# Gate products of two attentions on another engine, and a third buffer for the input tiles of a LayerNorm

## The chip, the cores and the metric

One core of a Trainium2 chip runs the whole layer. Five engines work beside each other, each with its own queue of instructions that it takes strictly in order: PE multiplies matrices (PEld loads its weights), DVE (VectorE) and ACT (ScalarE) do elementwise work, POOL (GpSimd) does slower elementwise work, and SP issues the transfers (DMA). An instruction that waits on a semaphore holds everything behind it in its queue. The metric is the device time of one execution in microseconds (us), the median of repeated runs.

## The reference

One layer of a streaming encoder, in float32: 1024 frames of width 1024, eight heads of width 64 in each of two attentions. Cut to what matters here:

```python
h = layer_norm(x, ln_in_g, ln_in_b)
proj = h @ w_in[0] + b_in[0]
a_q, a_k, a_v, a_z, b_cq, b_ckv, b_kr, b_z, g_a, g_b = split(proj)
ya = chunked_relpos_attention(a_q, a_k, a_v, rel_bias)   # 64-frame chunks, 8 chunks to the left
ya = (ya * silu(a_z)) @ w_proj_a
cq, ckv = rms_norm(b_cq), rms_norm(b_ckv)                # low-rank queries, keys and values
yb = chunk_causal_attention(q_full(cq), k_full(ckv, b_kr), v(ckv))
yb = (yb * silu(b_z)) @ w_proj_b
out = (sigmoid(g_a) * ya + sigmoid(g_b) * yb) @ w_out
h = layer_norm(2 ** 0.25 * h + out, ln_post_g, ln_post_b)
```

The gate products of the title are `ya * silu(a_z)` and `yb * silu(b_z)`.

## The kernel before

Every float32 matrix product is made of three passes over a high and a low part of each operand (`three`, L173 to L175); a helper `split` makes the parts (L131 on ACT for the high one, L132 on DVE or POOL for the low one).

**Opening.** x comes in eight tiles of 128 frames. For each, `ln_tile` takes statistics on DVE (L342, L344), the reciprocal root on POOL (L128, tile `rs`), centres and scales on DVE (L347, L350, in place in `xt`), stores the tile to `h_d` (L351), and turns it with PE transposes (L357, tile `hps`) into `hT`, high part by ACT (L358) and low part by DVE (L359). PE meanwhile multiplies the tiles that are ready into values (`v_tile`, tile `vps`). The x tiles live in a ring `x4` of four buffers, two of which hold the LayerNorm's rows `lng` and `lnb`; so two x tiles are in flight, and the load of tile 2 waits until tile 0 is stored. The same ring later holds the tiles `ct` of the low-rank projections, the tables `csT` and the tiles `qrt` of the rotated queries; a ring `str` of two half-size buffers holds `krh`, `krl`, `qrh` and `qrl`.

**Low-rank projections.** `c_tile` multiplies into `cps` (two PSUM buffers), DVE adds a bias (L407), ACT squares into the same PSUM tile (L410, L411), and only then may PE reuse it. DVE also computes the sine tables there (L466 to L494).

**Attention.** 64 steps for each of the two attentions (8 heads by 8 blocks of 128 queries). A step: PE scores (L712, L713, or L809 to L811), DVE evicts them with the row minimum (L717 or L816), ACT exponentiates (L828), DVE takes a reciprocal (L830, L831), ACT and DVE make the high and low half of the probabilities (L835, L836), SP issues a transposing transfer `pT<-p` (L838), and three (first attention) or two steps later PE multiplies `pT` with the values (L850, tile `y`). After every fourth step `finish_y` joins two halves of `y` into `yt` (L741 on ACT, L742 on DVE), and `finish_z` multiplies it by its gate `sz` (L748) and stores it to `y_d` (L750), 28 of 32 times; the last four are split on chip. Between the steps PE works through the dense projections (tile `dn`, weights `wr_c`, `wh_c`, `wl_c`), so that the latency of a step has dense work to hide behind.

**What sets the order.** Nobody writes the queues out: the kernel is traced under a scheduler that simulates a timeline and gives each engine its instructions in the order in which they become ready there. `tc.issue_after(i)` keeps the work inside it behind instruction i. A changed duration or buffer in one place therefore reorders the queues in many.

Of the kernel before, what the change touches and what calls it, by code (L numbers as in the profile page):

```python
# [11 lines left out]
F32R = mybir.dt.float32r  # L12
I32 = mybir.dt.int32
AF = mybir.ActivationFunctionType
ALU = mybir.AluOpType
# [3 lines left out]
P = 128  # L19
# [36 lines left out]
def tile_hybrid_layer(  # L56
# [25 lines left out]
    V, A, G, SY = nc.vector, nc.scalar, nc.gpsimd, nc.sync  # L82
# [220 lines left out]
    p0 = ctx.enter_context(ExitStack())  # L303
    p0w = ctx.enter_context(ExitStack())
    pw = p0.enter_context(tc.tile_pool(name="pw", bufs=1, side="right"))
    px = p0.enter_context(tc.tile_pool(name="px", bufs=4, side="right"))
    ln_p[0] = p0.enter_context(tc.tile_pool(name="ln_p", bufs=6, side="right"))
    pr = p0w.enter_context(tc.tile_pool(name="pr", bufs=8, side="right"))
    if True:
# [13 lines left out]
        lnb = px.tile([P, D], F32, tag="x4", name="lnb")  # L323
# [14 lines left out]
        def ln_tile(j):  # L338
            xt = xts.pop(j)
            st6 = ln_p[0].tile([P, 2, 6], F32, tag="st6", name=f"st6_{j}")  # L340
            for i in range(2):
                V.bn_stats(st6[:, i, :], xt[:, i * 512 : i * 512 + 512])  # L342
            mv = ln_p[0].tile([P, 2], F32, tag="mv", name=f"mv_{j}")
            V.bn_aggr(mv, st6)  # L344
            rs = ln_p[0].tile([P, 1], F32, tag="rs", name=f"rs_{j}")
            i_pool = rsqrt(rs, mv[:, 1:2], 1.0, 1e-5, 1, f"ln{j}")
            V.scalar_tensor_tensor(xt, xt, mv[:, 0:1], lng, op0=ALU.subtract, op1=ALU.mult)  # L347
            for b in range(2) if j == 0 else [slice(0, D)]:
                cs = slice(b * 512, b * 512 + 512) if j == 0 else b
                V.scalar_tensor_tensor(xt[:, cs], xt[:, cs], rs, lnb[:, cs], op0=ALU.mult, op1=ALU.add)  # L350
            SY.dma_start(h_d[j * P : (j + 1) * P, :], xt)  # L351
            sl = slice(j * P, (j + 1) * P)
            pool, tag = ((ps_sc, "sc"), (ps_y, "y"))[j % 2]
            for b in range(2):
                ps = pool.tile([P, 4, P], F32, tag=tag, name=f"hps{j}_{b}")
                for k in range(4):
                    i_pe = T.transpose(ps[:, k, :], xt[:, (4 * b + k) * P : (4 * b + k + 1) * P], ident).ins  # L357
                i_act = A.activation(hT[0][b][:, :, sl], ps, AF.Copy).ins  # L358
                i_dve = V.tensor_tensor(hT[1][b][:, :, sl], ps, f(hT[0][b][:, :, sl]), op=ALU.subtract).ins  # L359
            return i_pool, i_act, i_dve, i_pe  # L360

        dma_last = [None]

# [64 lines left out]
        def c_transpose(q):  # L428
            sl = slice(q * 512, q * 512 + 512)
            for b in range(4):  # L430
# [9 lines left out]
                    A.activation(dh, psf, AF.Copy, scale=g)  # L440
                    V.scalar_tensor_tensor(dl, psf, g, f(dh), op0=ALU.mult, op1=ALU.subtract)
                else:
                    kh = px.tile([32, 512], F32R, tag="str", name=f"krh{q}", bufs=2)
                    kl = px.tile([32, 512], F32R, tag="str", name=f"krl{q}", bufs=2)
                    A.activation(kh, psf[:32, :], AF.Copy)
                    V.tensor_tensor(kl, psf[:32, :], f(kh), op=ALU.subtract)
                    SY.dma_start(kr_d[0][:, sl], f(kh))
# [110 lines left out]
        ln_last = {}  # L558
# [14 lines left out]
        for j in range(2, NT):  # L573
            if j + 1 < NT:
                x_load(j + 1)
            ln_last[j] = ln_tile(j)
            v_tile(0, j - 1, w0)
            v_tile(1, j - 2, w1)
        v_tile(0, 7, w0)
# [42 lines left out]
    def rot_q(csT):  # L622
# [3 lines left out]
        for half in range(2):  # L626
# [7 lines left out]
            for a in range(2):  # L634
# [2 lines left out]
                V.tensor_tensor(t0, pss[a], csT[0][:, sl], op=ALU.mult)  # L637
                V.tensor_tensor(t1, pss[1 - a], csT[1][:, sl], op=ALU.mult)
                V.tensor_tensor(t0, t0, t1, op=ALU.subtract if a == 0 else ALU.add)
                hi = px.tile([P, 512], F32R, tag="str", name=f"qrh{a}{half}", bufs=2)  # L640
                lo = px.tile([P, 512], F32R, tag="str", name=f"qrl{a}{half}", bufs=2)
                split(t0, hi, lo)
                SY.dma_start(qr_d[0][a * P : (a + 1) * P, sl], f(hi))
                SY.dma_start(qr_d[1][a * P : (a + 1) * P, sl], f(lo))
# [2 lines left out]
    with ExitStack() as p1:  # L647
# [97 lines left out]
        def finish_z(pair, mixer, e, half, yt, r):  # L745
            h = 2 * pair.p + e
            sl = slice(half * 512, half * 512 + 512)
            G.tensor_tensor(yt[r, :], yt[r, :], pair.sz[half][r, :], op=ALU.mult)  # L748
            if h < 6 or mixer == 0:
                SY.dma_start(y_d[mixer][h * 64 : h * 64 + 64, sl], yt[r, :])  # L750
            else:
# [426 lines left out]
```

## Time and profile before

| | us |
|---|---|
| median of 3 runs (lowest, highest) | 878.96 (878.48, 880.91) |
| profiled execution, its own time | 874.21 |
| its span, first to last instruction | 872.4 |
| PE busy in the span | 821.9 |
| DVE busy | 592.2 |
| ACT busy | 443.0 |
| POOL busy | 197.6 |

The profiled execution is one run; the 1.8 us between its time and its span lie outside the instructions. PE is the engine to watch: what it waits for is what a change can win. In the rows below, a name in the form `out<-in` gives the tile that is written and those that are read; a bracket `[idle <-releaser]` says how long the engine had stood idle before the instruction and what ended that.

### The profile page before, as it was taken

Reading aid. Unit: us, or ns where it says so; the run is one execution under the profiler, and the core shown is the slowest. Engines: PE = TensorE matmul, PEld = TensorE weight load, DVE = VectorE, ACT = ScalarE, POOL = GpSimd, SP = SyncE. Lnnn points to the kernel's source line nnn. Section 1 sums busy time; section 2 is a strip of 40 time slices with the busy share of each in tenths; the row PEclk is TensorE's granted clock in tenths of the full one; section 3 lists DMA queues with packets and bytes.
Section 4 is the critical chain, followed back from the end, with each engine's and each line's share of the span. In section 5 each row is a group of like instructions: output and inputs, shape, how many; then the busy total and the mean of one; then the engine's idle time right before and its main releaser. Section 6 shows DMA issues by size and latency. Waiting matters only on the chain. (4 is left out here: it accounts for less than half of the span.)

```text
span 872.4 us, 13717 instructions
## 1 busy us (share of the span) xinstructions
PE 821.9 (94%) x4760; PEld 691.5 (79%) x4760; DVE 592.2 (68%) x1351; ACT 443.0 (51%) x857; POOL 197.6 (23%) x205
## 2 busy tenths in 40 slices
PE   5999999998998998999999999999999989999996
PEld 4999898887776876787778778787888778888886
DVE  6899856587686889845565767276637674647755
ACT  4223683476675857755563666366647552322000
POOL 6545630011111113400000521010213131331100
PEclk8999999999999999999999999999999999999999
DMA  6622023476877775674639377746886798541421
GB/s 210 209 106 77 13 62 109 142 149 141 165 138 168 139 178 96 135 202 102 152 96 200 80 166 159 162 102 140 192 199 173 186 217 289 161 151 49 160 94 48
DMA packets 185365, 124.68 MB, mean 143 GB/s; under 512 B 146161, under 2 KB 149745, under 8 KB 185297
## 3 DMA queue, kind: packets, MB, share of 16 engines
q1 hardware_dynamic: 185296, 123.82, 57.0%
q8 instruction: 37, 0.61, 0.3%
q14 instruction: 32, 0.25, 0.1%
HBM read 57.98 MB, written 22.81 MB: 93 GB/s over the span
## 5 line engine op out<-in xcount | busy, mean ns | idle before, releaser
L173 PE MATMUL dn<-hT,wh_c 128*128 128x512 f32 x512 | 204.8, 400 | 2.0 <-ACT g L294 1.3
L175 PE MATMUL dn<-hT,wl_c 128*128 128x512 f32 x512 | 201.5, 394 | 0.0
L174 PE MATMUL dn<-hT,wh_c 128*128 128x512 f32 x512 | 201.4, 393 | 0.0
L748 POOL TENSOR_TENSOR yt<-yt,sz 64x512 f32<-64x512 f32 x32 | 43.6, 1362 | 328.0 <-DVE yt L742 263.8
L173 PEld LDWEIGHTS dn<-hT,wh_c 128*128 128x128 f32 x512 | 97.0, 190 | 20.2 <-ACT g L294 1.8
L175 PEld LDWEIGHTS dn<-hT,wl_c 128*128 128x128 f32 x512 | 96.7, 189 | 20.0
L174 PEld LDWEIGHTS dn<-hT,wh_c 128*128 128x128 f32 x512 | 97.0, 189 | 17.6
L132 DVE TENSOR_TENSOR wl_c<-wr_c,wh_c 128x512 fp32r<-128x512 f32 x64 | 47.8, 746 | 77.4 <-ACT wh_c L131 71.2
L131 ACT ACTIVATE wh_c<-wr_c 128x512 fp32r<-128x512 f32 x64 | 40.2, 629 | 82.4 <-DMA wr_c<-in_wch_dram 63.2
L836 DVE SCALAR_TENSOR_TENSOR p<-sbs,rcs,p 128x128 f16<-128x128 f32 (+3 forms) x64 | 57.1, 901 | 24.2 <-ACT p L835 22.3
L828 ACT ACTIVATE sbs<-sbs,nmb 128x128 f32<-128x128 f32 (+3 forms) x64 | 49.5, 774 | 33.4 <-DVE sbs L816 30.1
L836 DVE SCALAR_TENSOR_TENSOR p<-ss,rcs,p 128x640 f16<-128x640 f32 (+2 forms) x64 | 50.7, 803 | 9.2 <-ACT p L835 8.1
L828 ACT ACTIVATE ss<-ss,nm 128x640 f32<-128x640 f32 (+2 forms) x64 | 44.3, 692 | 23.1 <-DVE nm L717 20.6
L835 ACT ACTIVATE p<-sbs,rcs 128x128 f16<-128x128 f32 (+3 forms) x64 | 48.5, 769 | 12.8 <-ACT sbs L828 6.8
L850 PE MATMUL y<-pT,v16b 128*128 128x128 f16 x576 | 43.7, 222 | 9.8 <-DMA pT<-p 9.8
L175 PE MATMUL ops<-wo,mixT 128*128 128x512 f32 (+1 forms) x144 | 52.9, 367 | 0.0
L850 PEld LDWEIGHTS <-v16b 128*128 128x128 f16 x576 | 33.9, 99 | 23.8 <-issue 22.2
L174 PE MATMUL ops<-wo,mixT 128*128 128x512 f32 (+1 forms) x144 | 52.7, 366 | 0.0
L173 PE MATMUL ops<-wo,mixT 128*128 128x512 f32 (+1 forms) x144 | 51.5, 368 | 0.0
L816 DVE TENSOR_SCALAR_CACHE_REDUCE sbs<-sb 128x128 f32<-128x128 f32 (+3 forms) x64 | 47.9, 754 | 1.3
L717 DVE CUSTOM_DVE_ANT_0 ss<-sa,tb 128x640 f32<-128x640 f32 (+2 forms) x64 | 41.3, 652 | 8.9 <-PE sa L713 5.2
L850 PE MATMUL y<-pT,v16a 128*128 128x128 f16 x480 | 37.4, 220 | 9.6 <-DMA pT<-p 9.6
(248 smaller groups left out, 1847.8 us busy)
## 6 DMA issues: line engine op xcount, KB each, us to landing
wr_c<-in_wch_dram SPq DMA_DIRECT2D x64, 256.0 KB, 3.2
th_d<-g SPq DMA_DIRECT2D x32, 256.0 KB, 2.9
th<-th_d SPq DMA_DIRECT2D x32, 256.0 KB, 3.7
h_d<-xt SPq DMA_DIRECT2D x8, 512.0 KB, 2.6
sX<-sQ SPq DMA_DIRECT2D x16, 256.0 KB, 4.2
sXb<-bQ SPq DMA_DIRECT2D x16, 256.0 KB, 4.3
r<-h_d SPq DMA_DIRECT2D x8, 512.0 KB, 3.6
wor<-in_wo_dram SPq DMA_DIRECT2D x16, 256.0 KB, 3.0
```

The source lines that it names most:

```text
L131: A.activation(hi, raw, AF.Copy)
L132: (eng or V).tensor_tensor(lo, raw, f(hi), op=ALU.subtract)
L173: T.matmul(ps, ah, bh, start=start, stop=False)
L174: T.matmul(ps, ah, bl, start=False, stop=False)
L175: return T.matmul(ps, al, bh, start=False, stop=stop).ins
L717: V.tensor_tensor_reduce(s[:, :n].rearrange("p (b w) -> p b w", b=nb), ps[:, :nb, :w], self.tb[e][:, 640 - n : 640].rearrange("p (b w) -> ...
L748: G.tensor_tensor(yt[r, :], yt[r, :], pair.sz[half][r, :], op=ALU.mult)
L816: V.tensor_scalar(s[:, :n].rearrange("p (b w) -> p b w", b=nb), ps[:, :nb, :w], -B_SCALE, None, op0=ALU.mult, op1=ALU.min, accum_out=nm,)
L828: A.activation(s[:, :n], s[:, :n], AF.Exp, scale=-1.0, bias=nm, accum_out=su)
L835: A.activation(hi, s[:, :n], AF.Copy, scale=rc2)
L836: V.scalar_tensor_tensor(lo, s[:, :n], rc2, hi, op0=ALU.mult, op1=ALU.subtract)
L850: T.matmul(o, v16[:, k0 + k, h % 4, :], pT[:, a * nk + k, :], start=(k == 0 and a == 0), stop=(k == nk - 1 and a == 1))
```

## The change

Three edits. The gate product `yt * sz` moves from POOL to DVE. The ring `x4` gets a fifth buffer, which makes three for x tiles, and the ring `str` goes: `krh`, `krl`, `qrh` and `qrl` take `x4` buffers (the memory is the same). And `ln_tile(j)` for j from 2 on is issued behind the last L350 of tile j-1, so that no statistics of a tile come before the scaling of the one ahead.

```diff
-    px = p0.enter_context(tc.tile_pool(name="px", bufs=4, side="right"))
+    px = p0.enter_context(tc.tile_pool(name="px", bufs=5, side="right"))
@@ ln_tile
-                V.scalar_tensor_tensor(xt[:, cs], xt[:, cs], rs, lnb[:, cs], op0=ALU.mult, op1=ALU.add)
+                i_sc = V.scalar_tensor_tensor(xt[:, cs], xt[:, cs], rs, lnb[:, cs], op0=ALU.mult, op1=ALU.add).ins
-            return i_pool, i_act, i_dve, i_pe
+            return i_pool, i_act, i_dve, i_pe, i_sc
@@ c_transpose
-                    kh = px.tile([32, 512], F32R, tag="str", name=f"krh{q}", bufs=2)
-                    kl = px.tile([32, 512], F32R, tag="str", name=f"krl{q}", bufs=2)
+                    kh = px.tile([32, 512], F32R, tag="x4", name=f"krh{q}")
+                    kl = px.tile([32, 512], F32R, tag="x4", name=f"krl{q}")
@@
         for j in range(2, NT):
             if j + 1 < NT:
                 x_load(j + 1)
-            ln_last[j] = ln_tile(j)
+            with tc.issue_after(ln_last[j - 1][4]):
+                ln_last[j] = ln_tile(j)
@@ rot_q
-                hi = px.tile([P, 512], F32R, tag="str", name=f"qrh{a}{half}", bufs=2)
-                lo = px.tile([P, 512], F32R, tag="str", name=f"qrl{a}{half}", bufs=2)
+                hi = px.tile([P, 512], F32R, tag="x4", name=f"qrh{a}{half}")
+                lo = px.tile([P, 512], F32R, tag="x4", name=f"qrl{a}{half}")
@@ finish_z
-            G.tensor_tensor(yt[r, :], yt[r, :], pair.sz[half][r, :], op=ALU.mult)
+            V.tensor_tensor(yt[r, :], yt[r, :], pair.sz[half][r, :], op=ALU.mult)
```

What moves in the queues, at three places. The first is DVE in the opening (xt_158 is x tile 1, xt_222 tile 2; L342 statistics, L350 scaling):

```order
 L127 TENSOR_SCALAR rst_ln_230<-mv_227 128x1
 L347 SCALAR_TENSOR_TENSOR xt_158<-xt_158,mv_227,lng 128x1024
-L342 BN_STATS st_2_299<-xt_222 128x6
 L350 SCALAR_TENSOR_TENSOR xt_158<-xt_158,rs_229,lnb 128x1024
-L342 BN_STATS st_2_299<-xt_222 128x6
+L342 BN_STATS st_2_299<-xt_222 128x6 x2
 L344 BN_AGGR mv_302<-st_2_299 128x2
```

The first half of tile 2's statistics no longer stands ahead of tile 1's scaling.

The second is SP in the opening (xt_124 is x tile 0, xt_297 tile 3; wv1r are weights of the second value group):

```order
 L121 DMA gkv<-in_kvn_g_dram 128x1
+L316 DMA xt_222<-in_x_dram 128x1024
+L351 DMA h_d<-xt_124 128x1024
 L458 DMA pi_t<-in_pos_dram 128x8
-L351 DMA h_d<-xt_124 128x1024
+L135 DMA wv1r_279<-in_wv_dram 128x512
 L459 DMA fr_t<-in_invf_dram 128x16
-L135 DMA wv1r_279<-in_wv_dram 128x512
 L135 DMA wv1r_283<-in_wv_dram 128x512
-L316 DMA xt_222<-in_x_dram 128x1024
+L316 DMA xt_297<-in_x_dram 128x1024
 L135 DMA wv1r_289<-in_wv_dram 128x512
```

The load of tile 2 now stands ahead of the store of tile 0, and every later x load one place earlier.

The third is DVE in the second attention, around the second product of its first head, before:

```order
L813 MEMSET sb_3_5366 64x64
L816 TENSOR_SCALAR sbs_2_5286,nmb_2_5287<-sb_2_5281 128x384
L742 SCALAR_TENSOR_TENSOR yt_0_1_5276<-y_0_4_5088,us_102,yl_0_1_5275 64x512
L816 TENSOR_SCALAR sbs_3_5371,nmb_3_5372<-sb_3_5366 128x512
L660 TENSOR_TENSOR bK_5173<-bk_1_5189,bK_5173 64x512
L830 TENSOR_SCALAR rcs_1_2_5291<-su_1_2_5289 128x1
```

and after (every line number behind L576 is one higher there):

```order
L743 SCALAR_TENSOR_TENSOR yt_0_1_5276<-y_0_4_5088,us_102,yl_0_1_5275 64x512
L814 MEMSET sb_4_5397 64x64
L831 TENSOR_SCALAR rcs_1_2_5291<-su_1_2_5289 128x1
L817 TENSOR_SCALAR sbs_3_5371,nmb_3_5372<-sb_3_5366 128x512
L749 TENSOR_TENSOR yt_0_1_5276<-yt_0_1_5276,sz_1_5042 64x512
L832 RECIPROCAL rcs_1_2_5291<-rcs_1_2_5291 128x1
L661 TENSOR_TENSOR bQ_5311<-bq_0_5313,bQ_5311 64x512
```

The product (L749) has joined DVE's queue, with an eviction and small work between it and the row that makes `yt`; the reciprocal of the step now stands behind it.

## Rows read from the trace of the kernel before

**Rows 1.** Page, busy us, share of the span and instructions of each engine.
```profile
PE 821.9 (94%) x4760; PEld 691.5 (79%) x4760; DVE 592.2 (68%) x1351; ACT 443.0 (51%) x857; POOL 197.6 (23%) x205
```
**Rows 2.** Stretches: length, busy PE, PEld, DVE, ACT, POOL, clock, DMA share, GB/s.
```profile
0.00:25.00 25.00, 14.49 (x80) 13.50 (x81) 17.17 (x23) 11.68 (x20) 17.34 (x19) 0.86 0.68 220
...
100.00:150.00 50.00, 50.00 (x262) 44.32 (x262) 31.71 (x95) 30.65 (x73) 13.05 (x20) 1.00 0.23 69
...
188.00:400.00 212.00, 198.70 (x1258) 163.64 (x1257) 158.01 (x380) 141.76 (x278) 41.46 (x49) 0.99 0.73 154
400.00:735.00 335.00, 318.92 (x1845) 261.23 (x1845) 206.67 (x512) 189.49 (x346) 55.18 (x47) 0.99 0.68 159
```
**Rows 3.** Timeline of PE: start us, duration us, instruction, [idle before <-releaser].
```profile
20.70 1.97 PE L357 MATMUL hps<-ident,xt 128*128 128x128 f32 x8 [4.53 <-DVE xt L350]
...
89.79 0.45 PE L173 MATMUL cps<-wcch,hT 128*128 128x416 f32 x1 [1.87 <-ACT cps L411]
```
**Rows 4.** Timeline of DVE in the opening.
```profile
15.42 1.28 DVE L347 SCALAR_TENSOR_TENSOR xt<-xt,mv,lng 128x1024 f32<-128x1024 f32 x1
18.09 0.69 DVE L342 BATCH_NORM_STATS2 st<-xt 128x6 f32<-128x512 f32 x1 [1.39 <-DMA xt<-in_x_dram]
18.70 1.95 DVE L350 SCALAR_TENSOR_TENSOR xt<-xt,rs,lnb 128x1024 f32<-128x1024 f32 x1
```
**Rows 5.** Timeline of POOL in the opening.
```profile
15.58 1.53 POOL L128 TENSOR_TENSOR rs<-rst_ln,mhalf 128x1 f32<-128x1 f32 x1 [0.48 <-DVE rst_ln L127]
17.09 2.48 POOL L132 TENSOR_TENSOR wv1l<-wv1r,wv1h 128x512 fp32r<-128x512 f32 x2
```
**Rows 6.** Timeline of PE, three waits in the attentions.
```profile
284.96 0.38 PE L850 MATMUL y<-pT,v16a 128*128 128x128 f16 x4 [2.40 <-DMA pT<-p]
...
337.59 0.42 PE L712 MATMUL sa<-sK,sQ 128*128 128x320 f32 x1 [2.28 <-DVE nm L717]
...
443.16 0.38 PE L809 MATMUL sb<-bK,bQ 128*128 128x320 f32 x1 [1.96 <-DVE sbs L816]
```
**Rows 7.** Busy time by stretch around waits; the granted clock stands third from the end.
```profile
20.00:24.00 4.00, 3.30 (x15) 3.07 (x16) 3.93 (x6) 1.21 (x3) 4.00 (x3) 0.57 0.67 224
282.00:288.00 6.00, 3.60 (x28) 2.93 (x27) 4.53 (x14) 5.07 (x11) 0.00 (x0) 1.00 0.78 119
336.00:340.00 4.00, 2.41 (x8) 2.13 (x9) 3.39 (x10) 2.38 (x5) 0.00 (x0) 0.73 0.42 98
```
**Rows 8.** Timeline of DVE, two later statistics in the opening.
```profile
27.86 1.29 DVE L342 BATCH_NORM_STATS2 st<-xt 128x6 f32<-128x512 f32 x2 [1.33 <-DMA xt<-in_x_dram]
...
39.91 1.29 DVE L342 BATCH_NORM_STATS2 st<-xt 128x6 f32<-128x512 f32 x2 [0.53 <-DMA xt<-in_x_dram]
```
**Rows 9.** Timeline of DVE, first bias of the low-rank projections.
```profile
88.11 0.58 DVE L407 TENSOR_TENSOR ct<-cps,bvc_t 128x416 f32<-128x416 f32 x1
```
**Rows 10.** Groups by line and form: count, busy us and mean ns, idle before.
```profile
L748 POOL TENSOR_TENSOR yt<-yt,sz 64x512 f32<-64x512 f32 x32 | 43.6, 1362 | 328.0 <-DVE yt L742 263.8
...
L132 DVE TENSOR_TENSOR YB<-yt,YB 64x512 fp32r<-64x512 f32 x4 | 2.7, 685 | 1.4 <-ACT YB L131 1.3
```
**Rows 11.** Waits: who waited for what, us in total, times, longest.
```profile
PE y L850 <- DMA pT<-p: 19.4, 23, 2.4
...
SPq L750 <- POOL yt L748: 17.8, 9, 3.7
```
**Rows 12.** Timeline of POOL and of SP around one product.
```profile
227.80 1.29 POOL L748 TENSOR_TENSOR yt<-yt,sz 64x512 f32<-64x512 f32 x1
...
229.12 0.46 SPq L750 DMA_DIRECT2D y_d<-yt  x1
229.68 1.27 SPq L838 DMA_TRANSPOSE pT<-p  x1
```
**Rows 13.** Tile wl_c, durations min/median/max; timeline of DVE beside a product.
```profile
L132 DVE TENSOR_TENSOR wl_c<-wr_c,wh_c x64: 673/692/1679, 80.8 to 647.8; 128x512 fp32r<-128x512 f32 x64
...
214.50 1.58 DVE L132 TENSOR_TENSOR wl_c<-wr_c,wh_c 128x512 fp32r<-128x512 f32 x1
```

## The prediction

> **What bounds the kernel now.** The first view is busy time by engine. PE is busy 821.9 of the 872.4 us of the span, 94% [rows 1]; no other engine comes near it. So the matrix products, which the change leaves alone, are a floor, and the 50 us in which PE stands idle, with the times at which its clock is low, are all that there is to win. The second view, busy time by stretch, says where they are [rows 2]: 10.5 us in the first 25 us, 13.3 us in the first attention (212 less 198.7) and 16.1 us in the second (335 less 318.9), while between 100 and 150 us PE has no gap at all. The third, PE's timeline, says what each gap waits for. In the opening the largest is 4.53 us for the scaling of x tile 1 by DVE, and at 89.79 us there are 1.87 us for ACT, which squares a tile of the low-rank projections [rows 3]. In the attentions most of the gaps end with a transposed tile of probabilities: 23 waits, 19.4 us [rows 11]; others end with an eviction by DVE [rows 6].
>
> The forecast is made as a difference. The profiled execution took 874.21 us, 872.4 of them span, and the median of the three timed runs is 878.96, so this one execution lies 4.75 us below the median; I take the terms from its rows and set the difference against the median.
>
> **The order of statistics, and the third buffer.** In the opening DVE centres tile 1 (start 15.42, 1.28 us, to 16.70), then stands 1.39 us for the arrival of tile 2, takes half of tile 2's statistics (18.09, 0.69 us), and only then scales tile 1, from 18.70 [rows 4]. The scaling needs the root from POOL, which was there at 15.58 + 1.53 = 17.11 [rows 5]. With the statistics behind it, it starts at 17.11: 18.70 - 17.11 = 1.6 us earlier. Its own 1.95 us against the 1.28 us of the centring, an instruction of the same form, could shrink too, since a POOL instruction on two SBUF tiles starts at 17.09 beside it [rows 4, 5]; as that is still there, I keep 1.95 us and hold 0.67 us as a bound. PE has waited for nothing else there, so its first gap falls from 4.53 to 2.9 us. Term: -1.6, between -1.6 and -2.3.
>
> The earlier load of tile 2 is costed at nothing: it goes out behind the loads of the first weights and of tile 1, and the DMA engines are busy 0.68 of this stretch [rows 2]. What it is now ahead of is the store of tile 0 and the second group's weights, which PE needs only after tile 1. If this cover fails, 512 KB at the stretch's 220 GB/s [rows 2] are 2.4 us, an estimate, and the 1.6 us are gone.
>
> **The clock behind the gap.** From 20 to 24 us the granted clock is 0.57 [rows 7]: PE runs most of this at 1.2 and not 2.4 GHz, after standing still for 4.53 us. That costs 4 x 0.43 = 1.7 us. Whether a gap of 2.9 us brings the fall is open: behind the 2.28 us at 337.59 the clock fell (0.73 over 336 to 340), behind the 2.40 us at 284.96 it did not (1.00) [rows 6, 7]. One row each way: I take half, -0.85, between 0 and -1.7.
>
> **What is late next.** Later statistics also stood for their x tile, 1.33 and 0.53 us [rows 8]; with the loads one place earlier I expect these waits to go. With the 1.39 us that is 3.3 us of DVE idle time, and PE, full from here on, cannot use it directly. It counts at 89.79, where PE's 1.87 us end with ACT, ACT with DVE's bias at 88.11 [rows 3, 9], and DVE comes from a long queue of tables. PE gets there 1.6 us sooner. If DVE gets there sooner by the whole 3.3 us, the gap shrinks by 1.7 us, nearly all; if by no more than PE, it stays. DVE's last low part of `hT` needs PE's last transpose, so it is tied to PE in part; I take the middle, -0.9, between 0 and -1.7.
>
> The sharing of one ring by `krh` to `qrl` and the `qrt` tiles makes the second rotated pair wait for the first. I cost it at nothing: between 100 and 150 us PE is busy 50.00 of 50.00 us with dense work [rows 2]. Without that cover it would be a wait for a reused PSUM buffer, of the size of the 1.87 us [rows 3].
>
> **The products.** There are 32, 1.36 us each on POOL, which mostly stood waiting for them [rows 10]. On DVE the nearest row is `YB`, a product-like instruction of the same 64x512 form with both inputs in SBUF: 0.685 us [rows 10]. So DVE gets 32 x 0.69 = 22 us more in the two attentions, where it is busy 158.0 + 206.7 of 547 us [rows 2], 67%. On the average this fits. The question is the step's chain, where DVE acts four times between scores and transfer. Behind a product in DVE's queue stand evictions, reciprocals and low halves; ACT waits for these, then SP's transposing transfer, then PE.
>
> Upper bound: a product delays the steps then in DVE's queue, two of them with the lag of two or three, so 64 of the 128; half of the 23 waits for `pT` then grow by 0.69: +7.9 us. Lower bound: SP, which issues all transfers in one queue, stood 9 times, 17.8 us in all, for POOL's product before it could store it [rows 11], and the next transposing transfer stood right behind the store: product to 229.09, store at 229.12, transfer at 229.68 [rows 12]. A product that takes 0.69 and not 1.29 us frees SP 0.6 us sooner: 9 x 0.6 = -5.4 us, if every one were in PE's way. Both fail for the same reason, that most of this time is hidden, and I see nothing that decides between them: term 0, both ends kept for the range.
>
> There is a second gain on DVE: beside a product on POOL, the low part `wl_c` took 1.58 us where 0.69 is its median [rows 13]; eviction rows, which read PSUM, do not show this. The Trainium skill, in "SBUF — State Buffer", section "Who interferes with whom", says that a VectorE instruction with two SBUF inputs and a GpSimd instruction that reads SBUF exclude each other, the later one waiting for the whole of the first. By that rule alone up to 32 x 1.36 = 43 us of DVE time could come back, and the product on DVE could itself be held by what stays on POOL; the rows agree on the lock, but a median of 0.69 against a least of 0.67 [rows 13] says that it is met seldom. I leave it in the term of 0, since DVE is not what bounds.
>
> **Sum.** -1.6 - 0.85 - 0.9 + 0 = -3.35 us; 878.96 - 3.35 = 875.6 us. A measurement of this kernel can tell about 0.3%, 2.6 us, from no change: the limits are 876.3 and 881.6.
>
> **The rivals.**
> - *The opening is given back.* PE comes 1.6 us sooner to 89.79, but DVE's tables are no earlier, because POOL's instructions slow them as they slow the 1.95 us row; the gap grows to 3.5 us, and the clock falls in the opening as before. For: DVE is idle little there. Against: 3.3 us of DVE waits are removed upstream. Time: 879.0, or 877.4 with the gap unchanged.
> - *Slower: the products stand before the reciprocals.* One mechanism, on DVE in the attentions, at up to +7.9 us. With the opening's sure -1.6: 878.96 - 1.6 + 7.9 = 885.3. It decides from (2.6 + 1.6) / 0.69, six of the 23 waits. For: the order after shows a reciprocal right behind a product, next to an eviction for which PE waited 1.96 us [rows 6]. Against: between `yt` and the product other rows were placed, so it seldom waits for its input, and half of the steps have slack.
> - *Faster by more.* SP's queue was what made transposes late. -2.3 - 1.7 - 1.7 - 5.4 = -11.1: 867.9. For: 17.8 us of standing. Against: in most of the nine the tile behind was not one that PE waited for, by the totals.
>
> **How the numbers follow.** The forecast, 873 to 876.3, gets 0.34; no change 0.34; slower 0.18; faster by more 0.14. So faster by over 0.3% 0.48, within 0.3% 0.34, slower 0.18. The range leaves out the far ends of the last two: 870 to 882.5. As cases of both signs hold much of the chance, the forecast's own range stands beside it: 873 to 876.3.
>
> **What would show it.** In the changed profile: tile 1's scaling at about 17.1 and PE's transposes behind it at about 19.1 (if still near 20.7, the first term is wrong); the granted clock of 20 to 24 us; the wait before the third low-rank tile, which should be below 1.87 us at about 87; x waits of DVE near zero; product rows on DVE of 0.69 us; PE's idle time in the two attentions near 29 us in all, and its waits for `pT` near 19 us. If these rise to 25 or more, the slower rival holds. The forecast is wrong above all if the new order moves gaps about in the attentions by more than I allow, since every queue there was dealt anew.

## The result, and the profile after

The changed kernel is slower: 891.67 us (median of 4 runs, 891.11 to 893.85) beside 878.72 us for the kernel before (median of 4). The ratio is 1.0155, with a 95% interval of 1.0118 to 1.0191, so 13 to 14 us. The forecast was 875.6 us, between 870.0 and 882.5.

The profiled execution took 891.75 us. Its page begins with the span and the busy time by engine (share of the span, instructions):

```profile
span 889.8 us, 13708 instructions
...
PE 831.7 (93%) x4760; PEld 697.1 (78%) x4760; DVE 604.9 (68%) x1383; ACT 443.2 (50%) x857; POOL 151.4 (17%) x173
```

Beside [rows 1], PE executes the same 4760 instructions in 9.8 us more busy time (831.7 less 821.9), and its idle time grows from 50.5 to 58.1 us, by 7.6. Together that is the 17.4 us by which the two spans differ (889.8 less 872.4). More busy time for the same products is the clock. So in this pair of profiles more than half of the loss is clock, and less than half is waiting. The profiled execution of before lay 4.75 us under its median, so the spans overstate the difference, and the clock's share as well: the mean granted clock on record is 0.979 in the four timed runs of the changed kernel and 0.985 to 0.987 in the runs of the kernel before that stood beside the experiments. Over spans of 890 and 878 us that is some 6 of the 13 us, an estimate.

Busy time by stretch says where (length, busy PE, PEld, DVE, ACT, POOL, granted clock, DMA share, GB/s), first after, then the last stretch of before, which [rows 2] do not have:

```profile
0.00:25.00 25.00, 16.14 (x86) 14.88 (x87) 18.26 (x25) 11.58 (x20) 17.31 (x19) 0.82 0.75 251
...
188.00:400.00 212.00, 201.19 (x1274) 165.66 (x1272) 160.17 (x397) 142.01 (x279) 20.47 (x34) 0.98 0.71 155
400.00:735.00 335.00, 312.50 (x1785) 253.95 (x1784) 213.64 (x522) 187.13 (x343) 31.39 (x30) 0.98 0.65 148
640.00:760.00 120.00, 105.40 (x571) 84.04 (x570) 69.63 (x154) 52.76 (x93) 16.49 (x13) 0.96 0.71 188
```

```profile
640.00:760.00 120.00, 115.43 (x638) 93.61 (x637) 75.47 (x158) 56.74 (x101) 31.18 (x23) 1.00 0.76 204
```

The opening and the first attention hold more PE work than in [rows 2] (16.14 against 14.49 us, 201.19 against 198.70). The second attention holds less (312.50 against 318.92), above all its end: between 640 and 760 us PE is busy 105.40 us, not 115.43, and gets through 571 instructions, not 638. The two profiles can also be set beside each other by the work that PE has done, the matrix columns that its instructions have moved so far. By this measure the changed kernel is level with before at 400 us and 3 us ahead at 500. It then falls back by 5 us up to 520, by 7 between 640 and 720 and by 9 between 720 and 740, and ends 17 us behind. PE's timeline of after has these gaps (start, duration, instruction, [idle before <-releaser]):

```profile
18.11 1.09 PE L357 MATMUL hps<-ident,xt 128*128 128x128 f32 x8 [3.01 <-DVE xt L350]
...
90.35 0.46 PE L173 MATMUL cps<-wcch,hT 128*128 128x416 f32 x1 [2.69 <-ACT cps L411]
...
515.64 1.65 PE L851 MATMUL y<-pT,v16b 128*128 128x128 f16 x14 [3.06 <-DMA pT<-p]
...
704.12 0.27 PE L851 MATMUL y<-pT,v16b 128*128 128x128 f16 x2 [3.69 <-DMA pT<-p]
...
747.47 0.76 PE L173 MATMUL pj<-YB,wh_p 128*128 128x512 f32 x1 [5.07 <-DVE ya L254]
```

and behind each of them the granted clock (third from the end) falls to about 0.5, the lower of its two levels, 1.2 instead of 2.4 GHz (in the second and the fourth of these stretches only for a part, 0.61 and 0.72):

```profile
20.00:24.00 4.00, 3.83 (x18) 3.83 (x19) 3.52 (x4) 1.12 (x3) 3.85 (x3) 0.50 0.53 150
90.00:94.00 4.00, 3.65 (x13) 3.42 (x14) 3.00 (x27) 3.03 (x11) 2.16 (x4) 0.61 0.00 0
514.00:520.00 6.00, 4.36 (x22) 3.97 (x22) 2.56 (x13) 3.34 (x9) 0.00 (x0) 0.51 0.97 212
704.00:710.00 6.00, 5.88 (x23) 4.59 (x23) 3.37 (x10) 2.37 (x5) 0.96 (x1) 0.72 0.68 197
746.00:752.00 6.00, 4.53 (x11) 3.59 (x12) 1.89 (x3) 0.00 (x0) 0.00 (x0) 0.52 1.03 398
```

The last three cost most. Those at 704 and 747 us are new, and the one at 515 us has doubled, from 1.45 us. Each has its story in a queue.

**The gap at 747 us** ends with DVE's product of a projection block with its gate tile `th`, for which DVE had waited 3.72 us. SP's queue shows why the tile was late (start, duration, instruction, count):

```profile
730.69 4.11 SPq L839 DMA_TRANSPOSE pT<-p  x2
734.91 5.08 SPq L135 DMA_DIRECT2D wr_p<-in_wpb_dram  x2
740.09 4.23 SPq L239 DMA_DIRECT2D th<-th_d  x8
```

The loads of `th` stand behind the last two transposing transfers and behind two loads of weights that wait for buffers, 5.08 us. In the kernel before, the order at this place is much the same:

```profile
716.06 3.20 SPq L838 DMA_TRANSPOSE pT<-p  x1
719.36 4.66 SPq L135 DMA_DIRECT2D wr_p<-in_wpb_dram  x2
724.11 3.92 SPq L239 DMA_DIRECT2D th<-th_d  x8
```

The two loads of weights take 4.66 us there too, but PE came to the gate tiles only at 732.8 us and found them. What has changed is that the last transposes, and all that stands behind them, go out late.

**The gap at 515 us** begins on ACT, some 8 us earlier. After, and then before:

```profile
507.41 0.69 ACT L294 ACTIVATE g<-dn,bcolh 128x512 f32<-128x512 f32 x1 [2.31 <-DMA y_d<-yt]
508.00 1.14 ACT L829 ACTIVATE sbs<-sbs,nmb 128x1024 f32<-128x1024 f32 x1
```

```profile
506.49 1.13 ACT L828 ACTIVATE sbs<-sbs,nmb 128x1024 f32<-128x1024 f32 x1
509.70 0.67 ACT L294 ACTIVATE g<-dn,bcolh 128x512 f32<-128x512 f32 x1
```

The gate `g` and the `yt` tiles share one ring of five buffers (`st`). The scheduler has put `g` ahead of the exponential of step 7; `g` waits 2.31 us until the store of a `yt` has landed, and the exponential, which waits for nothing there, stands behind it, then the probabilities, SP's transpose and PE. The Trainium skill, in "PSUM — Partial Sum Buffer", section "Engine vs sequencer instructions", calls the queue of ScalarE a strict first in, first out; these rows agree: a ready exponential did not pass a waiting gate. In the order of ACT's instructions the swap is one line:

```
490 L828 ACTIVATE sbs2_7_6018,su1_2_7_6021<-sbs2_7_6018,nmb2_7_6019 128x1024
491 L835 ACTIVATE p161_2_6_5955<-sbs2_6_5947,rcs1_2_6_5952 128x896
...
493 L294 ACTIVATE g10_0_6055<-dn_24_0_5993,bcolh_98 128x512
```

before, and after:

```
490 L294 ACTIVATE g10_0_6055<-dn_24_0_5993,bcolh_98 128x512
491 L829 ACTIVATE sbs2_7_6018,su1_2_7_6021<-sbs2_7_6018,nmb2_7_6019 128x1024
492 L836 ACTIVATE p161_2_6_5955<-sbs2_6_5947,rcs1_2_6_5952 128x896
```

**The gap at 704 us** waits for the last head's first probabilities, in a part of the queues in which the scores of the last head come later among the projection blocks than before. PE's waits for `pT`, split by attention, tell more than the total of [rows 11] did (us, times, longest; the first attention is 188 to 400 us, the second 400 to 735). Before:

```profile
PE y L850 <- DMA pT<-p: 8.8, 11, 2.4
PE y L850 <- DMA pT<-p: 9.8, 11, 1.9
```

After:

```profile
PE y L851 <- DMA pT<-p: 4.5, 7, 1.4
PE y L851 <- DMA pT<-p: 15.5, 13, 3.7
```

The total hardly moves (20.0 us in 20 waits). The first attention has halved, and the second has grown by more than half.

### The profile page after: what moved, and what is told of

It reads as the page before. It is cut to its first block, busy times and chain, and to the rows that moved or that the text cites. A ratio compares the mean times of both kernels' runs of the same rounds, so it can differ in the third digit from the quotient of the medians.

```text
span 889.8 us, 13708 instructions
## 1 busy us (share of the span) xinstructions
PE 831.7 (93%) x4760; PEld 697.1 (78%) x4760; DVE 604.9 (68%) x1383; ACT 443.2 (50%) x857; POOL 151.4 (17%) x173
## 5 line engine op out<-in xcount | busy, mean ns | idle before, releaser
L132 DVE TENSOR_TENSOR wl_c<-wr_c,wh_c 128x512 fp32r<-128x512 f32 x64 | 45.5, 711 | 81.9 <-ACT wh_c L131 77.8
L837 DVE SCALAR_TENSOR_TENSOR p<-sbs,rcs,p 128x128 f16<-128x128 f32 (+3 forms) x64 | 56.8, 890 | 17.8 <-ACT p L836 15.8
L851 PE MATMUL y<-pT,v16b 128*128 128x128 f16 x576 | 44.3, 222 | 15.6 <-DMA pT<-p 15.5
L837 DVE SCALAR_TENSOR_TENSOR p<-ss,rcs,p 128x640 f16<-128x640 f32 (+2 forms) x64 | 46.9, 750 | 8.1 <-ACT p L836 7.5
L836 ACT ACTIVATE p<-ss,rcs 128x640 f16<-128x640 f32 (+2 forms) x64 | 42.5, 688 | 8.7 <-DMA pT<-p 3.4
```

The lines of the kernel that those rows point to most:

```text
L132: (eng or V).tensor_tensor(lo, raw, f(hi), op=ALU.subtract)
L836: A.activation(hi, s[:, :n], AF.Copy, scale=rc2)
L837: V.scalar_tensor_tensor(lo, s[:, :n], rc2, hi, op0=ALU.mult, op1=ALU.subtract)
L851: T.matmul(o, v16[:, k0 + k, h % 4, :], pT[:, a * nk + k, :], start=(k == 0 and a == 0), stop=(k == nk - 1 and a == 1))
```

## The experiments

**The theories.** *Opening*: the third buffer and the ordered statistics lose the time. *Price*: each product costs its 0.69 us in DVE's queue, ahead of reciprocals and low halves. *Order*: the products as such cost little, but with them the scheduler deals the queues of the second attention anew, and a few waits land in bad places. All ratios below are to the kernel before, with 95% intervals.

**Which part, which attention.** Four kernels take the change apart: the products alone (e1), the opening's edits alone (e2), and the opening with the products of one attention (e3, e4). The edit is one line in `finish_z`; for e3:

```
-            V.tensor_tensor(yt[r, :], yt[r, :], pair.sz[half][r, :], op=ALU.mult)
+            (V if mixer == 0 else G).tensor_tensor(yt[r, :], yt[r, :], pair.sz[half][r, :], op=ALU.mult)
```

e1: 

> The kernel before with its 32 products on VectorE and nothing else changed. Its order at the end of the second attention is that of the changed kernel: the transposing transfers of the last head's steps 2 to 5 stand behind the reloads of the second mixer's y and behind two loads of weights. Theory 'order' (the loss comes from where the products of the second mixer push the last head): the loss of 640 to 750 us is there in full, total 890 to 893 us against some 879. Theory 'price' (each product costs VectorE's queue its 0.69 us): a loss spread over both attentions, total 884 to 892, with more waits for transposed probabilities than 20 us. Theory 'opening' (the third buffer and the ordered statistics lose the time): no loss, 877 to 881.

e2: 

> The changed kernel with its products back on GpSimd: the third buffer, the shared ring and the ordered statistics alone. Its order at the end of the second attention is that of the kernel before. Theory 'order': no loss there; the opening's gain is given back by 110 us as in the changed kernel, total 876 to 880. Theory 'price': the same, 876 to 880. Theory 'opening': 889 to 893. If merely any newly dealt queues cost time by chance: anything within 10 us, with gaps in the attentions at other places than in either kernel.

e3: 

> The changed kernel with the 16 products of the second mixer back on GpSimd; those of the first mixer stay on VectorE. The order at the end of the second attention is that of the kernel before. Theory 'order': no loss at 640 to 750 us, total 876 to 880. Theory 'price': half of the loss of the changed kernel, 884 to 886, in the first attention. Theory 'opening': 889 to 893.

e4: 

> The changed kernel with the 16 products of the first mixer back on GpSimd; those of the second stay on VectorE. The order at the end of the second attention is that of the changed kernel. Theory 'order': the whole loss, nearly all of it between 640 and 750 us, total 889 to 893. Theory 'price': half of it, 884 to 886. Theory 'opening': 889 to 893 too, but e2 and e3 then as slow.

| kernel | median us | ratio (interval) | PE busy in 640 to 760 us |
|---|---|---|---|
| e1, products alone | 895.75 | 1.0170 (1.0133 to 1.0208) | 104.11 |
| e2, opening alone | 876.76 | 0.9960 (0.9936 to 0.9984) | 115.30 |
| e3, opening and first 16 products | 872.55 | 0.9922 (0.9890 to 0.9955) | 116.65 |
| e4, opening and second 16 products | 893.08 | 1.0138 (1.0099 to 1.0178) | 104.90 |

The opening is cleared. The whole loss belongs to the 16 products of the second mixer: with those of the first on POOL they cost 1.78%, 16 us (e4 less e2), with those of the first on DVE 2.33%, 20 us (the changed kernel less e3). As many instructions in the first attention cost nothing; e3 is, if anything, faster than e2 (the intervals overlap), and PE's waits for `pT` between 160 and 400 us are 5.2 us in e3 and 8.6 us in e2. e3 beats both kernels. A price of 0.69 us for each product would have put e3 and e4 alike, so *price* in its plain form is out; *order* named the place, 640 to 760 us, though not every size: e1 came out 3 us above its 890 to 893, e3 some 3 us below its 876 to 880.

**Order or price, at the end of the second attention.** e5 keeps all 32 products on DVE and holds PE's order by hand; e6 gives e3, which has none of these products on DVE, a late last head; e7 and e8 add to e3 two products each, of head 6 and of head 7.

```
+        with tc.issue_after(last_sc[0]) if m == 0 and d >= 2 else nullcontext():   # e5, in proj
             for k in range(4):
                 three(ps, wh[:, k, :], wl[:, k, :], YT[m][0][k][:, sl], YT[m][1][k][:, sl], k == 0, k == 3)
```

```
-            i = min(left, key=lambda i: done[i] / total[i] / (LEAD if i == 0 else 1))
+            i = min(left, key=lambda i: done[i] / total[i] / ((lead_[0] or LEAD) if i == 0 else 1))   # e6: lead_[0] = 0.85 in the last run
```

e5: 

> The changed kernel with all 32 products on VectorE, and TensorE's order at the end of the second attention held by hand: the projections of the first mixer from their third block on are queued behind the scores that stand before them in the code. The last head's steps 2 to 4 thus come before block 2 and in it, as in the kernel before; in the changed kernel step 2 comes behind block 2 and most of block 3. Theory 'order' (the late last head is the loss, not the products): no late loads at 740 us, total 868 to 876. Theory 'price' (16 products in VectorE's queue cost some 20 us in the second attention, wherever the scores stand): 886 to 893.

e6: 

> e3 (the second mixer's products on GpSimd, 872.6 us) with one number changed, the lead of the attention over the projections in the last stretch, 0.85 and not 1.25: the last head's step 2 now stands behind all of block 2 of the projections, and steps 3 to 7 further back than in e3. Theory 'order': the loss appears without any product on VectorE there, 880 to 893, with waits for transposed probabilities and late loads behind 740 us. Theory 'price': as e3, 870 to 875.

e7: 

> e3 with two more products on VectorE, those of head 6 of the second mixer. The order at the end turns into one like the changed kernel's: the last head's step 2 behind block 2 and all of block 3's first half. Theory 'order': nearly the whole loss, 884 to 893. Theory 'price': 2 products of 0.69 us, 872 to 875.

e8: 

> e3 with two more products on VectorE, those of head 7, the last, whose path to the end is the shortest. The order at the end stays as in the kernel before. Theory 'order': as e3, 870 to 875. Theory 'price': as e7, since it is the same work, and 1 to 3 us above e3 if the last product stands in the way of the last splits.

| kernel | median us | ratio (interval) |
|---|---|---|
| e5, all on DVE, heads first | 885.21 | 1.0065 (1.0038 to 1.0093) |
| e6, late last head, products on POOL | 876.78 | 0.9967 (0.9939 to 0.9995) |
| e7, e3 and two products of head 6 | 880.13 | 1.0000 (0.9974 to 1.0026) |
| e8, e3 and two products of head 7 | 873.34 | 0.9918 (0.9891 to 0.9945) |

The pair e7 and e8 is the clearest, although e7 came out at 880.13 us, between the 884 to 893 of *order* and the 872 to 875 of *price*. Two instructions more cost 7 us in one case (0.82%) and nothing in the other. What differs is the order: with head 6's products on DVE the end of the queues turns into one like the changed kernel's. PE's and DVE's rows of e7 show the late loads of `th` again:

```profile
730.40 0.76 PE L173 MATMUL pj<-YB,wh_p 128*128 128x512 f32 x1 [5.30 <-DVE ya L254]
```

```profile
729.57 0.69 DVE L254 SCALAR_TENSOR_TENSOR ya<-th,pj 128x512 f32<-128x512 f32 x1 [5.89 <-DMA th<-th_d]
```

e5 gives back 0.9%, 8 us, by order alone, and its trace has no gap before the projections of the second mixer; but at 1.0065 it misses its 868 to 876 by 9 us or more. e6 loses 0.45% against e3 where 1 to 2% was expected, and the intervals overlap: its last scores come 12 us later than e3's (714.5 and 702.2 us), and most of that hides behind the projection blocks, which it does earlier instead. So a late last head is not the loss; a late last head with late loads behind it is. *Order* holds for about half of the loss, and the other half was open.

**Single places.** e9 has 26 products on DVE, those of heads 5 to 7 of the second mixer on POOL, and SP's order at the end as before. e10 to e12 are the changed kernel with places held by hand: weights behind the gate loads (e10), two transfers behind transposes (e11), and both of these with e5's edit (e12).

```
+        with tc.issue_after(last_th[0]) if m == 1 and d >= 2 else nullcontext():   # e10, in prep_p
             wq_[m, d] = load_w((wpa, wpb)[m][d], f"p{m}{d}")
```

```
+        with tc.issue_after(tr["1_6_4"]) if (m, d) == (0, 3) else nullcontext():   # e11, in prep_p
             wq_[m, d] = load_w((wpa, wpb)[m][d], f"p{m}{d}")
...
+        with tc.issue_after(tr["1_6_5"]) if (m, d) == (0, 2) else nullcontext():   # e11, in load_th
             SY.dma_start(th, th_d[m][d * P : (d + 1) * P, sl])
```

e9: 

> The changed kernel with 26 of its 32 products on VectorE: all of the first mixer and those of heads 0 to 4 of the second; heads 5 to 7 of the second go back to GpSimd. SyncE's queue at the end of the second attention is that of the kernel before. Theory 'order': as e3, 870 to 875, since products as such cost nothing. Theory 'price' (the products of the second mixer cost their time wherever the queues stand): ten of the sixteen are on VectorE, so ten sixteenths of the 18 us between e3 and e4, 882 to 886.

e10: 

> The changed kernel, all 32 products on VectorE, with one load of weights (the third block of the second mixer's projection) queued behind the gate loads that TensorE needs first. The gap of 5.07 us at 747 us, which waits for these loads, should shrink by the 2.5 us that the second load of weights held SyncE's queue, or to nothing if the next loads then stand early enough, and the clock behind it should not fall: 3 to 7 us of the 9 us lost at 725 to 745 us, so 885 to 889. If the gap has another cause, for instance the last low halves of y, the time stays at 891 to 893.

e11: 

> The changed kernel with two transfers moved in SyncE's queue to where the kernel before has them: one load of weights behind the transposing transfer of head 6, step 4, and two gate loads behind that of step 5. If the loss of 645 to 700 us (6.5 us) comes from transposes that stand behind loads which wait for a free buffer, it is gone: 885 to 888. If it comes from the products in VectorE's queue, 891 to 893.

e12: 

> The changed kernel, all 32 products on VectorE, with the order held in the three places together: scores of the last head first (e5), weights behind the gate loads (e10), transposes before loads (e11). Theory 'order': 870 to 878, near e3. Theory 'price': no lower than e5, 884 to 890.

| kernel | median us | ratio (interval) |
|---|---|---|
| e9, 26 products | 879.51 | 1.0012 (0.9983 to 1.0042) |
| e10, weights behind loads | 888.52 | 1.0140 (1.0074 to 1.0206) |
| e11, transposes first | 889.20 | 1.0140 (1.0111 to 1.0168) |
| e12, all three | 883.39 | 1.0087 (1.0058 to 1.0117) |

e10 shows its mechanism and not its worth. SP's and PE's rows:

```profile
734.63 4.01 SPq L841 DMA_TRANSPOSE pT<-p  x2
738.74 0.99 SPq L135 DMA_DIRECT2D wr_p<-in_wpb_dram  x1
739.82 3.72 SPq L241 DMA_DIRECT2D th<-th_d  x8
```

```profile
747.69 0.47 PE L173 MATMUL pj<-YB,wh_p 128*128 128x512 f32 x1 [1.39 <-DVE ya L256]
```

From the end of the transposes to the gate loads it is 1.2 us now, 5.3 in the changed kernel, and the gap falls from 5.07 to 1.39 us. By the work that PE has done, e10's profile wins 6 us on the changed kernel's at this place. The median lies in the range expected for it, but it cannot be told from the changed kernel's: in this execution the queues had come to that place some 4 us later, and the interval is wide. e11 failed: 1.0140, against 885 to 888 us expected, so the loads ahead of those two transposes were not what cost the time at 645 to 700 us. e12 is no better than e5, and with 883.39 us it misses the 870 to 878 of *order*. And e9, with before's order at the end, still loses 0.9% against e3 and lies between its two ranges; of this *order*, as I had put it, knew nothing. Its trace has the wait of ACT for a store, and PE's wait behind it:

```profile
504.26 0.69 ACT L294 ACTIVATE g<-dn,bcolh 128x512 f32<-128x512 f32 x1 [2.10 <-DMA y_d<-yt]
```

```profile
512.46 1.65 PE L851 MATMUL y<-pT,v16b 128*128 128x128 f16 x14 [3.04 <-DMA pT<-p]
```

In the profiles read for it, that ACT wait is there wherever the products of heads 0 to 4 are on DVE with the gate in that place (after, e1, e4, e5 and e9 to e12: 0.3 to 2.9 us, once in each), and nowhere where they are on POOL (before, e2, e3, e6 to e8). But a late tile at this place has other causes too. In e8, which has the gate where before has it and is as fast as e3, PE waits longer than in e9:

```profile
516.84 1.17 PE L851 MATMUL y<-pT,v16b 128*128 128x128 f16 x14 [3.43 <-DMA pT<-p]
```

There the gate stands on ACT behind a weight part that waits 1.83 us for its load, and SP's transposes stand behind the store of the gate. So the wait in one profile does not tell what the place costs.

**One instruction moved, and the opening's term by itself.** e13 is e9, and e14 is e12, with that one gate queued behind step 6's probabilities; the other queues keep their order but for some twenty instructions in all. e15 is the kernel before with the ordered statistics alone.

```
+            with tc.issue_after(ph["1_2_6"]) if (m, d, half) == (1, 0, 0) else nullcontext():
                 A.activation(t, ps, AF.Tanh, scale=0.5, bias=bcolh[:, c : c + 1])
```

e13: 

> e9 (26 products on VectorE, 1.001 of the kernel before) with one ScalarE instruction moved: the gate g of the second mixer's first block is queued behind head 2's step 6 probabilities, as in the kernel before, and not ahead of step 7's exponential. In e9 it waits 2.1 us for the store of a y tile, whose buffer it takes over, and the exponential, the low half, the transposing transfer and TensorE (3.04 us) wait behind it, after which the clock is low. Theory 'one wait in one queue': the 3.04 us shrink to below 2 and the clock stays up, 3 to 5 us, so 0.996 to 0.998 of the kernel before. Theory 'price of the products': as e9, 1.001.

e14: 

> e12 (all 32 products on VectorE, order held in three places, 1.009 of the kernel before) with the same ScalarE instruction moved. Theory 'waits in queues': another 3 to 5 us, so 1.003 to 1.006. What then remains above e3's 0.992 would be waits at places not held here, above all that of 3.67 us at 689 us of e12. Theory 'price of the products': as e12, 1.009.

e15: 

> The kernel before with the ordered statistics alone: products on GpSimd, four buffers for x, the ring of two kept. All queues stay as in the kernel before but for the opening. The forecast's opening term by itself: 1.6 us at the first gap and up to 1.7 us of clock, 0.996 to 0.998. If the gain of e2 (0.996) comes from the buffer and the shared ring, 0.999 to 1.001.

| kernel | median us | ratio (interval) |
|---|---|---|
| e13, e9 with the gate moved | 876.09 | 0.9966 (0.9933 to 0.9999) |
| e14, e12 with the gate moved | 881.03 | 1.0018 (0.9985 to 1.0051) |
| e15, ordered statistics alone | 879.72 | 1.0003 (0.9973 to 1.0033) |

Moving one ACT instruction of 0.7 us is worth 0.46% in e13 and 0.69% in e14 by the ratios, 4 and 6 us; 3 to 5 us had been expected of each. The intervals of e9 and e13 overlap by a little, and the bare medians differ by only 3.4 and 2.4 us, since each pair ran beside other runs of the kernel before. So the worth is 2 to 6 us. In e13's profile ACT's wait is gone, and PE's wait and the clock follow:

```profile
505.51 0.67 ACT L296 ACTIVATE g<-dn,bcolh 128x512 f32<-128x512 f32 x1
```

```profile
512.22 0.94 PE L853 MATMUL y<-pT,v16b 128*128 128x128 f16 x14 [2.22 <-DMA pT<-p]
```

The clock between 510 and 518 us is 0.79 there and 0.59 in e9. That accounts for 2 to 3 us. In e14 ACT's wait is gone too, but PE's falls only from 3.05 to 2.79 us, since the two transposes took 5.77 us and not 4.13, and the two profiles as a whole, with spans of 880.3 (e12) and 880.0 us, do not differ. So the gain is measured by the ratios; its whole size is not found at this one place in single profiles. e15 says that the ordered statistics alone are worth nothing that can be measured; a gain of up to 2.4 us lies within its interval.

**What is left.** e14 has all 32 products on DVE and, with the order held in four places, has come from the 1.0155 of the changed kernel to 1.0018. It is still 0.96% above e3. Its profile shows where: by the work that PE has done it is 2 us behind e3's at 640 us and 9 us at 720, of 10 at the end. The longest of PE's waits there, with the clock at 0.50 from 688 to 694 us, is this:

```profile
688.01 1.65 PE L860 MATMUL y<-pT,v16b 128*128 128x128 f16 x14 [3.70 <-DMA pT<-p]
```

No run moved what this tile waits for. e16 asks whether sixteen more instructions in DVE's queue cost time when no store and no buffer waits for them.

```
+            if mixer == 1:
+                V.tensor_tensor(scr[r, :], pair.sz[half][r, :], pair.sz[half][r, :], op=ALU.mult)
             (V if mixer == 0 else G).tensor_tensor(yt[r, :], yt[r, :], pair.sz[half][r, :], op=ALU.mult)
```

e16: 

> e3 (0.992 of the kernel before; the second mixer's products on GpSimd) with 16 more VectorE instructions of the product's form, one for each product of the second mixer, which multiply a gate by itself into a tile that nobody reads; no result of the kernel changes. VectorE carries the same 32 instructions of 0.69 us as in the changed kernel, but no store and no buffer waits for the added 16. The queues are dealt once more, in an order that is neither e3's nor the changed kernel's: the last head's steps 2 to 4 stand between the reloads of y. Theory 'waits in queues': 870 to 878, 0.990 to 0.998, moved only by what the new order does. Theory 'price of the products': 16 times 0.69 us in the second attention, 11 us above e3, so 1.004 or more.

It took 882.03 us, 1.0075 (1.0043 to 1.0106), 1.5% above e3: *price* had said 1.004 or more, *order* 0.998 at most. But the loss isn't spread over sixteen instructions. Set against e3's by the work that PE has done, its profile is 3 us behind at 610 us; it then falls back by 4 us near 620 and by 7 near 675, regains 3 to 4 by 700, and ends 10 us behind. At the last of these places DVE, ACT, SP and PE show:

```profile
672.52 1.38 DVE L751 TENSOR_TENSOR scr<-sz 64x512 f32<-64x512 f32 x2
673.93 0.15 DVE L834 TENSOR_SCALAR rcs<-su 128x1 f32<-128x1 f32 x1
...
676.12 1.00 DVE L840 SCALAR_TENSOR_TENSOR p<-sbs,rcs,p 128x768 f16<-128x768 f32 x1
```

```profile
674.37 0.94 ACT L839 ACTIVATE p<-sbs,rcs 128x768 f16<-128x768 f32 x1 [0.86 <-ACT yl L743]
```

```profile
673.06 3.48 SPq L239 DMA_DIRECT2D th<-th_d  x4
677.18 1.81 SPq L842 DMA_TRANSPOSE pT<-p  x1
```

```profile
682.01 1.44 PE L854 MATMUL y<-pT,v16b 128*128 128x128 f16 x12 [4.11 <-DMA pT<-p]
```

Two added rows stand ahead of a reciprocal, ACT's probabilities wait for it, the transpose goes out at 677.18, and PE waits 4.11 us, with the clock at 0.57 from 680 to 688. This is the mechanism of the prediction's rival, products before the reciprocals, seen at one place. The four loads ahead of the transpose did not hold it in SP's queue: they ended at 676.54, and the low half of the probabilities was ready only at 677.12. The two added rows take 1.38 us of DVE's time; how much of PE's 4.11 us they made, and how much the new order around them, no run parts.

## Why the prediction was wrong

**The opening.** The first step came as described. DVE's scaling of tile 1 is no longer behind statistics and starts at 15.78 us, earlier than the 17.11 forecast, as soon as POOL's root is there:

```profile
15.78 2.28 DVE L350 SCALAR_TENSOR_TENSOR xt<-xt,rs,lnb 128x1024 f32<-128x1024 f32 x1 [0.45 <-POOL rs L128]
```

```profile
14.22 1.53 POOL L128 TENSOR_TENSOR rs<-rst_ln,mhalf 128x1 f32<-128x1 f32 x1 [0.48 <-DVE rst_ln L127]
15.72 3.47 POOL L132 TENSOR_TENSOR wv1l<-wv1r,wv1h 128x512 fp32r<-128x512 f32 x2
```

PE's gap is 3.01 us where I said 2.9, and DVE's waits for later x tiles are gone. The second step fell on the bad side: the clock fell behind the smaller gap too, to 0.50, where [rows 7] had 0.57. In e3, with the same opening, the clock stays at 1.00 over these 4 us behind a gap of 2.64 us, so single executions differ here. The third failed: the wait before the third low-rank tile is 2.69 us, not below the 1.87 of [rows 3]. PE came there only 0.3 us earlier, and DVE's first bias 0.6 us later, at 88.74 and not at the 88.11 of [rows 9]; the clock fell behind this wait as well. That is the first rival, the opening given back. e15 (1.0003) agrees with it: its first gap is 2.99 us, as forecast, and then PE waits for DVE in the middle of the tables, where the kernel before has no wait:

```profile
82.29 0.50 PE L175 MATMUL dn<-hT,wl_c 128*128 128x512 f32 x1 [3.08 <-DVE wl_c L132]
```

All three opening edits together measured 0.9960 in e2, 3.5 us, the size of my sum, but not by my steps: in e2's profile the lead over before, by the work that PE has done, is 1.6 us at 80 us and 0.3 at 100. What is there came with the buffer, the ring that I had costed at nothing, or the queues dealt anew. That is left open, and the agreement in size is luck.

**The products, first attention.** The instruction's duration was right, and so was the average load, DVE being busy 68% as before. The tile's row gives the durations in ns, min/median/max:

```profile
L749 DVE TENSOR_TENSOR yt<-yt,sz x32: 666/687/1150, 191.6 to 740.8; 64x512 f32<-64x512 f32 x32
```

In the first attention PE's waits for `pT` halved, as the "faster by more" rival had it, but not by its mechanism. Of SP's standing, 17.8 us for POOL's products, 3.7 us for DVE's products is left in this view, which goes from 160 to 735 us:

```profile
SPq L751 <- DVE rcs L832: 6.7, 8, 1.7
SPq L751 <- DVE yt L749: 3.7, 4, 2.3
```

but all rows of SP's waits before these stores add up to 19.9 us: the names changed, the standing did not. What halved the waits is open.

**The products, second attention: the step that failed.** I took the term as 0 between -5.4 and +7.9 us. The 16 products of the second mixer cost 16 to 20 us (e4 against e2, the changed kernel against e3). The upper bound was mis-sized in three ways. It let a wait grow by the duration of one product, 0.69 us; the waits that came were 3.06, 3.69 and 5.07 us, since what is late is a whole chain: a gate that waits for a store, gate loads behind late transposes and weights. It priced no clock in the attentions, although [rows 7] had shown it fall behind a gap of 2.28 us; lower clock is 9.8 of the 17.4 us between the two profiles, and some 6 of 13 over the timed runs. And it kept the queues' order fixed apart from the products, though the text said that every queue was dealt anew: the one sentence that named this, the last, carried no price. The runs put about 8 us on the order at the end (e5 against the changed kernel; two products of head 6, 7 us), 2 to 6 us on one ACT instruction (e13, e14), and leave some 8 us (e14 against e3; the shares need not add up). Most of these lie between 640 and 720 us; what makes the tiles there late stays open, and e16 gives one mechanism and no proof.

**The slower rival.** It had the direction and the stage, at 0.18, but was too cheap. Its mechanism, a product ahead of a reciprocal on DVE, was seen only in e16; the gaps that were followed up stand behind ACT's queue and SP's. And its test could not see them: "waits for `pT` of 25 us or more". The total stayed at 20.0 us, because the first attention's fall hid the second's rise from 9.8 to 15.5.

## What to carry to other kernels

Where a scheduler deals the queues, an edit of 0.7 us is not priced by its duration: look in the new order, on each in-order queue, for an instruction that waits for a reused buffer or a store and now stands ahead of one on the critical chain, and price that by the whole chain and the clock behind the gap. Hold one such place by hand at a time to see what it is worth. Split every sum of waits by stage before using it as a test, since a gain in one stage hides a loss in another. Where work of one kind runs in two stages, move it in each by itself: the same edit limited to the first attention (e3) took 872.55 us, 0.9922 of the kernel before. The receiving engine's load does not say which stage it will be: by [rows 2] DVE was busy 75% of the first attention, where the products cost nothing, and 62% of the second.

## What the runs showed of the hardware

The clock made small gaps dear. PE's gap of 3.06 us was followed by 0.51 of the full clock over 514 to 520 us. In the kernel before, the wait at that place and the clock are these:

```profile
515.48 0.94 PE L850 MATMUL y<-pT,v16b 128*128 128x128 f16 x14 [1.45 <-DMA pT<-p]
```

```profile
514.00:520.00 6.00, 4.55 (x44) 3.97 (x43) 3.82 (x14) 2.75 (x8) 0.00 (x0) 1.00 0.83 187
```

The length of a gap alone did not decide: behind waits of 2.22 us (e13) and 2.71 us (e1) at the same place the clock was 0.79 (510 to 518 us) and 1.00 (516 to 526). In this pair of profiles lower clock took more time from PE than waiting did, 9.8 against 7.6 us. Two transposing transfers in a row, with no other transfer between them, took 2.5 to 5.8 us of SP's queue in the profiles of after and e14 (2.53 at 608 us of after, 5.77 at 507 us of e14), which is more than any product that was moved. DVE's scaling of x tile 1 took 2.28 us, with POOL's `wv1l` beside it, where the centring, an instruction of the same form, took 1.27 us just before it; the forecast had held it possible that this row shrinks from its 1.95 us, and it grew.
